# Stick-breaking attention: both heads' logits in one tile of two PSUM banks, weights scaled in halves

## The chip, the core and the metric

The kernel runs on one core of a Trainium2 chip. The metric is the device time of one launch in microseconds. TensorE (PE, with its weight loads as PEld), VectorE (DVE), ScalarE (ACT), GpSimd (POOL) and the DMA-issuing SyncE (SP) run side by side, each through its own queue in order, and wait for each other by semaphores.

## What is computed

A decoder trunk of two layers over 1040 tokens (16 meta tokens and 1024 of the sequence), width 1024, in float32: a Mamba-2 mixer and a gated FFN, then stick-breaking attention and a second gated FFN. The change touches the attention, 16 heads of 64:

```python
kv = _rmsnorm(h, kv_norm) @ w_kv
q = (_rmsnorm(h, sb_norm[j]) @ sb_w_q[j]).reshape(b, L, SB_HEADS, SB_HEAD_DIM)
...
logits = jnp.einsum('bthd,bshd->bhts', q[:, t0:t1], k[:, :t1]).astype(jnp.float32) * scale
visible = s_idx < t_idx
log_keep = jnp.where(visible, jax.nn.log_sigmoid(-logits), 0.0)
later = lax.cumsum(log_keep, axis=3, reverse=True) - log_keep
log_w = jnp.where(visible, jax.nn.log_sigmoid(logits) + later, -jnp.inf)
w = jnp.exp(log_w).astype(v.dtype)
outs.append(jnp.einsum('bhts,bshd->bthd', w, v[:, :t1]))
```

The kernel takes the sums of logarithms as running products: `kp` holds sigmoid(-logit) and is scanned from the right, `bt` holds sigmoid(logit) and is multiplied by the scanned `kp` of its right neighbour.

## The kernel before

Mixer, FFN and output projection are ordered by the framework's scheduler. The attention is written out by hand: on PE, DVE, ACT and POOL its instructions run in program order.

`attention` (L1385) goes through eight **pairs** of heads. A pair has 18 **steps** n = 0 to 17, one for each (i, jj): query block i of 116 tokens against the third jj of the keys (at most 348 columns), jj falling from i//3 to 0. The steps with jj = i//3, on the diagonal, are n = 0, 1, 2, 3, 5, 7, 9, 12 and 15. Steps 0, 3 and 9 have 116 columns, 1, 5 and 12 have 232, all others 344 or 348. In each step:

- `weigh` (L1317) computes the logits: for each of the two heads two matmuls into a PSUM bank of its own, `lg` (L1332; two banks in all). ACT takes from each bank a sigmoid into `kp` (L1335) and one into `bt` (L1336), the first head's two ahead of the second's. On the diagonal POOL masks both (L1341). DVE scans `kp` (L1345) and multiplies `bt` (L1346), head by head. POOL sets one column of each `kp` to 1 (L1329). `kp` has six buffers and `bt` eight, that is three and four steps.
- `half` (L1238) is half a projection: 12 matmuls of the weight tiles `wh`, `wl` against the normed tokens, into `pj` (L155 to L157; two banks, tag `mm`). Steps 0 to 7 project the last third of the pair's own v, q, k, v; steps 8 to 17 the first two thirds of the next pair's k, q, q, k and the first of its v, two steps for each. What reads a finished `pj` comes a step later in program order: for q two copies on ACT (L1279) and two subtractions on DVE (L1283, from `pj`), for k a copy (L1266) and a subtraction (L1267); ahead of these, in the same step, `pj` of k is read by DVE (L1255) and `pj` of v by ACT (L1257).
- A **chore**, where one is due. `load` (L1207) issues the DMA of a weight tile `w32` (128 x 1024) for the next pair at the end of step 4 (k), 7 (q) or 9 (v), and appends two chores, of which each following step runs one. A chore (`some`, L1226) takes half of the tile: four ACT copies with the norm's gain as scale make `wh` (L1233), four DVE operations make `wl` (L1234). Pair 0's own weights go through POOL.
- `flush` (L1398): `turn` (L1350) of the step three back, which transposes the weights `bt` (up to six transposes, L1359, into one of three `sm` banks for each head) and copies them to SBUF on ACT (L1363). When blocks 2b and 2b+1 are complete, `values` (L1365) multiplies with v (`po`, L1374), and ACT copies `po` out (L1381).

The last pair has no next pair to project: from step 8 on its steps hold logits, transposes and values alone, and PE has little to do in them. The eight PSUM banks are: `mm` 2, `lg` 2, `sm` 3, `ex` 1.

Of the kernel before, what the change touches and what calls it, by code (L numbers as in the profile page):

```python
# [68 lines left out]
class Trunk:  # L69
    def __init__(self, ctx, tc, a):  # L70
        self.tc, self.nc, self.a = tc, tc.nc, a
        nc = self.nc
# [4 lines left out]
        self.mp = ctx.enter_context(tc.tile_pool(name="mp", bufs=2, space=bass.MemoryType.PSUM))
        self.sp = ctx.enter_context(tc.tile_pool(name="sp", bufs=SMB, space=bass.MemoryType.PSUM))
        self.dp = ctx.enter_context(tc.tile_pool(name="dp", bufs=1, space=bass.MemoryType.DRAM))
        self.n = 0  # L80
# [14 lines left out]
    def mm(self, s="mm"):  # L95
        return self.mp.tile([P, 512], F32, tag="mm", name=self.nm(s))
# [4 lines left out]
    def lg(self, s="lg"):  # L101
        return self.sp.tile([P, 512], F32, tag="lg", name=self.nm(s), bufs=LGB)
# [1094 lines left out]
    def heads(self, u, p, pool):  # L1197
# [4 lines left out]
        class Pair:  # L1202
# [4 lines left out]
            def load(me, kind):  # L1207
# [18 lines left out]
                def some(k0):  # L1226

                    if k0 == 0:
                        me.w[kind] = [self.wp.tile([P, 1024], F32R, tag=t, name=self.nm(t)) for t in ("wh", "wl")]
                    for k in range(k0, k0 + KD // 2):  # L1230
                        w, wh, wl = (t[:, k * P : k * P + P] for t in (w32, *me.w[kind]))
                        g = self.par(gain, k)
                        nc.scalar.activation(wh, w, AF.Copy, scale=g)  # L1233
                        nc.vector.scalar_tensor_tensor(wl, w, g, wh.bitcast(F32), op0=ALU.mult, op1=ALU.subtract)  # L1234
# [82 lines left out]
    def weigh(self, i, jj, qd, ks, prev, pool):  # L1317
# [6 lines left out]
        out = []  # L1324
        for a in range(2):
            kp = pool.tile([P, TW], F32, tag="kp", name=self.nm("kp"), bufs=6)
            bt = pool.tile([P, TW], F32, tag="bt", name=self.nm("bt"), bufs=8)

            nc.gpsimd.memset(kp[:nt, m : m + 1], 1.0)  # L1329
            ps = self.lg()  # L1330
            for x, part in enumerate(qd[a]):
                nc.tensor.matmul(ps[:nt, :m], part[:, c0 : c0 + nt], ks[a][:, s0 : s0 + m], start=x == 0, stop=x == 1)  # L1332
            out.append((kp, bt, ps))
        for kp, bt, ps in out:
            nc.scalar.activation(kp[:nt, :m], ps[:nt, :m], AF.Sigmoid, scale=self.rt[2][:nt, i : i + 1])  # L1335
            nc.scalar.activation(bt[:nt, :m], ps[:nt, :m], AF.Sigmoid, scale=self.rt[1][:nt, i : i + 1])  # L1336
        for a, (kp, bt, _) in enumerate(out):
            if jj == j:

                for t, fill in ((kp, 1.0), (bt, 0.0)):  # L1340
# [4 lines left out]
            nc.vector.tensor_tensor_scan(rev, rev, self.one[:nt].to_broadcast([nt, m + 1]), init, ALU.mult, ALU.mult)  # L1345
            nc.vector.tensor_tensor(bt[:nt, :m], bt[:nt, :m], kp[:nt, 1 : m + 1], op=ALU.mult)  # L1346
            prev[a] = kp
        return [bt for _, bt, _ in out]
# [185 lines left out]
    def run(self, ctx):  # L1534
        tc = self.tc
        with tc.tile_pool(name="mx", bufs=1) as mx:
            hd, ys, yd = self.mixer(mx)
        self.rp = ctx.enter_context(tc.tile_pool(name="rp", bufs=1))
        with tc.tile_pool(name="ff0", bufs=2) as pool:
            d, *forms = self.out_proj(hd, ys, yd, pool)  # L1540
            g = self.up(0, *forms, pool)
            h1 = self.dp.tile([KD, P, L], F32, tag="h1_d", name="h1_d")

            def to_attention(h, j, u):
                u = self.norm(h, j, u)
                self.spill_tile(h, h1, *TT[j])
                return u

            u = self.down(0, g, d, pool, to_attention)
        with tc.tile_pool(name="att", bufs=2) as pool:  # L1550
# [3 lines left out]
        with tc.tile_pool(name="ff1", bufs=2) as pool:  # L1554
# [65 lines left out]
```

## Time and profile before

| | us |
|---|---|
| median of 3 runs | 2925.82 (2924.74 to 2927.37) |
| the profiled execution | 2925.94 |
| its span, first to last instruction | 2924.2 |
| mixer and first FFN: 0 to 1578 | 1578, PE busy 1534.4, DVE 1109.3, ACT 878.9 |
| attention: 1578 to 2118 | 540, PE busy 517.7, DVE 452.1, ACT 427.5, POOL 129.6 |
| output projection and second FFN: 2118 to the end | 806, PE busy 784.2, DVE 565.6, ACT 392.6 |

Busy times are unions of instructions, and matmuls overlap: two of the same kind start 0.16 us apart and are shown with 0.32 us each. So a stall of PE shows best as a longer distance from one start to the next, or as idle time of PEld, and less as idle time of PE. Timeline rows give start, duration, engine, line, operation and tiles; a number in brackets at the end is the engine's idle time just before, with what ended it.

### The profile page before, as it was taken

What the parts mean: (1) busy time and instruction counts of PE and PEld (TensorE: products, weight loads), DVE (VectorE), ACT (ScalarE), POOL (GpSimd) and SP (SyncE); (2) the same over time, 40 slices, a digit from 0 to 9 for tenths busy, and PEclk for the clock granted to TensorE, in tenths of its full rate; (3) what the DMA queues carried; (4) which work ended last, traced back from release to release, by engine and by line L of the source; (5) the groups of instructions that cost most, each with busy time, mean ns of one, the idle gap of its engine ahead of it and who ended that gap; (6) DMA issues with size and microseconds to landing.
All of it is one profiled execution on the core that took longest, in us unless ns stands there. A gap on an engine that the chain in (4) does not pass through costs nothing.

```text
span 2924.2 us, 57048 instructions
## 1 busy us (share of the span) xinstructions
PE 2836.3 (97%) x21793; PEld 2705.8 (93%) x21793; DVE 2127.0 (73%) x4100; ACT 1699.1 (58%) x3608; POOL 700.9 (24%) x956
## 2 busy tenths in 40 slices
PE   8999999999999999999999999999898999999998
PEld 5999898988998999999998999999797999999888
DVE  5685858776497655558986888888869656557895
ACT  5586667763155555555335888787736555555442
POOL 0000000000005666650002222222200766662000
PEclk9999999999999999999999999999999999999999
DMA  4233333323222222235132222222341222225331
GB/s 166 71 110 93 115 92 106 112 66 135 75 94 66 81 81 78 76 117 198 52 127 72 64 60 64 61 68 54 98 163 48 86 78 80 80 80 188 108 108 59
DMA packets 133570, 272.74 MB, mean 93 GB/s; under 512 B 16400, under 2 KB 68240, under 8 KB 133296
## 3 DMA queue, kind: packets, MB, share of 16 engines
q1 hardware_dynamic: 127984, 258.17, 27.8%
q10 hardware_dynamic: 4048, 6.36, 0.6%
q0 software_dynamic: 1264, 4.57, 0.4%
q8 instruction: 171, 2.80, 0.4%
q14 instruction: 103, 0.84, 0.1%
HBM read 200.93 MB, written 53.21 MB: 87 GB/s over the span
## 4 chain that ended last, share of the span: by engine, by line
PE 65%; DVE 7%; ACT 4%; issue 1%; DMA 1%; ACTq 0%; DVEq 0%; POOL 0%; SPq 0%; POOLq 0%
PE p L155 9%; PE p L157 9%; PE p L156 9%; PE acc L156 8%; PE acc L157 8%; PE acc L155 8%; PE po L1374 2%; PE pj L155 2%; PE pj L157 2%; PE pj L156 2%; PE lg L1332 2%; PE wT L1359 1%; DVE kp L1345 1%; ACT kp L1335 1%; ACT bt L1336 1%
## 5 line engine op out<-in xcount | busy, mean ns | idle before, releaser
L155 PE MATMUL pj<-uh,wh 128*128 128x348 f32 (+2 forms) x1536 | 504.1, 329 | 17.5 <-DVE xbc L278 9.1
L156 PE MATMUL pj<-ul,wh 128*128 128x348 f32 (+2 forms) x1536 | 496.9, 324 | 0.0
L157 PE MATMUL pj<-uh,wl 128*128 128x348 f32 (+2 forms) x1536 | 494.5, 322 | 0.0
L155 PE MATMUL p<-bh,fh 128*128 128x262 f32 (+1 forms) x1408 | 399.1, 284 | 12.3 <-DVE p L969 6.8
L156 PE MATMUL p<-bl,fh 128*128 128x262 f32 (+1 forms) x1408 | 399.5, 284 | 0.9 <-DVE bl L854 0.7
L157 PE MATMUL p<-bh,fl 128*128 128x262 f32 (+1 forms) x1408 | 398.5, 284 | 0.7 <-DVE fl L919 0.7
L155 PEld LDWEIGHTS pj<-uh,wh 128*128 128x128 f32 x1536 | 290.4, 189 | 25.6 <-issue 11.5
L155 PE MATMUL p<-bh,wh 128*128 128x262 f32 (+1 forms) x1056 | 301.0, 285 | 1.9 <-ACT bh L853 1.7
L156 PE MATMUL p<-bl,wh 128*128 128x262 f32 (+1 forms) x1056 | 300.0, 284 | 2.1 <-DVE bl L854 2.1
L157 PE MATMUL p<-bh,wl 128*128 128x262 f32 (+1 forms) x1056 | 299.5, 284 | 0.0
L156 PEld LDWEIGHTS pj<-ul,wh 128*128 128x128 f32 x1536 | 290.9, 189 | 1.0
L157 PEld LDWEIGHTS pj<-uh,wl 128*128 128x128 f32 x1536 | 290.5, 189 | 0.3 <-issue 0.2
L155 PEld LDWEIGHTS p<-bh,fh 128*128 128x128 f32 x1408 | 267.1, 190 | 13.8 <-DVE p L969 7.2
L278 DVE SCALAR_TENSOR_TENSOR c<-p,params,c 128x260 f32<-128x260 f32 (+1 forms) x440 | 208.4, 482 | 92.6 <-ACT c L274 90.8
L156 PEld LDWEIGHTS p<-bl,fh 128*128 128x128 f32 x1408 | 267.2, 190 | 2.5 <-DVE bl L854 2.4
L157 PEld LDWEIGHTS p<-bh,fl 128*128 128x128 f32 x1408 | 266.2, 189 | 1.1 <-DVE fl L919 1.1
L919 POOL TENSOR_TENSOR fl<-x,fh 128x1024 fp32r<-128x1024 f32 x80 | 192.3, 2404 | 246.8 <-ACT fh L918 246.8
L969 DVE TENSOR_TENSOR p<-p,ft 128x262 f32<-128x262 f32 (+1 forms) x176 | 76.4, 436 | 215.6 <-ACT ft L966 123.1
L156 PE MATMUL acc<-gl,wh 128*128 128x260 f32 (+1 forms) x672 | 211.5, 320 | 0.1
L157 PE MATMUL acc<-gh,wl 128*128 128x260 f32 (+1 forms) x672 | 208.8, 320 | 0.0
L155 PE MATMUL acc<-gh,wh 128*128 128x260 f32 (+1 forms) x672 | 204.0, 319 | 0.0
L156 PEld LDWEIGHTS p<-bl,wh 128*128 128x128 f32 x1056 | 200.7, 190 | 3.1 <-DVE bl L854 3.1
(313 smaller groups left out, 7717.3 us busy)
## 6 DMA issues: line engine op xcount, KB each, us to landing
w<-in_w_up SPq DMA_DIRECT2D x88, 512.0 KB
w<-in_w_down SPq DMA_DIRECT2D x44, 512.0 KB
w<-in_w_in SPq DMA_DIRECT2D x40, 512.0 KB
E<-ea_d SPq DMA_DIRECT2D x32, 464.0 KB
D<-acs_d SPq DMA_DIRECT2D x32, 420.5 KB
g<-c SPq DMA_DIRECT2D x88, 130.0 KB
g<-c SPq DMA_DIRECT2D x88, 128.0 KB
b<-g SPq DMA_DIRECT2D x16, 520.0 KB
```

The costliest lines, as they stand in the source:

```text
L155: mm(out, wh, uh, start=first, stop=False, skip_group_check=joins)
L156: mm(out, wh, ul, start=False, stop=False, skip_group_check=joins)
L157: mm(out, wl, uh, start=False, stop=last, skip_group_check=joins)
L278: nc.vector.scalar_tensor_tensor(to, ps[:, o + i : o + i + n], wcol(i), out, op0=ALU.mult, op1=ALU.add)
L919: tt(lo[:, :n], t, hi[:, :n].bitcast(F32), op=ALU.subtract)
L969: add = lambda o, x, y: tt(o[:, :N], x[:, :N], y[:, :N], op=ALU.add)
L1332: nc.tensor.matmul(ps[:nt, :m], part[:, c0 : c0 + nt], ks[a][:, s0 : s0 + m], start=x == 0, stop=x == 1)
L1335: nc.scalar.activation(kp[:nt, :m], ps[:nt, :m], AF.Sigmoid, scale=self.rt[2][:nt, i : i + 1])
L1336: nc.scalar.activation(bt[:nt, :m], ps[:nt, :m], AF.Sigmoid, scale=self.rt[1][:nt, i : i + 1])
L1345: nc.vector.tensor_tensor_scan(rev, rev, self.one[:nt].to_broadcast([nt, m + 1]), init, ALU.mult, ALU.mult)
L1359: nc.tensor.transpose(pt[:ns, x * CB : x * CB + nt], bt[a][:nt, x * CB : x * CB + ns], self.ident[:nt, :nt])
L1374: nc.tensor.matmul(po[64 * a : 64 * a + 64, w], v[: CH[c][1], c, 64 * a : 64 * a + 64], wt[a][: CH[c][1], c, :nt], start=x == 0, stop=x == ...
```

## The change

In the attention `lg` becomes one tile of two banks, `lg2`, with a head in each, and one such tile in place of two banks. One sigmoid for `kp` and one for `bt` now take both heads at once, as do the mask, the column of ones and the product. The two scans stay. `kp` has three double tiles and `bt` four. The chores of pairs 1 to 7 change: the first multiplies the whole weight tile by the gain in place, in two halves on DVE; the second makes `wh` in two ACT copies and `wl` in two DVE subtractions. The load of q moves from step 7 to step 6. In the last pair, from step 9 on, odd steps take a second `lg2` tile, in the two banks that the projections had. To allow this the banks `mm` and `lg` come from pools (`banks`) that are opened for each stage.

```diff
-        self.mp = ctx.enter_context(tc.tile_pool(name="mp", bufs=2, space=bass.MemoryType.PSUM))
...
+    def banks(self):
+        return self.tc.tile_pool(name=self.nm("lp"), bufs=1, space=bass.MemoryType.PSUM)
...
-                def some(k0):
-
-                    if k0 == 0:
-                        me.w[kind] = [self.wp.tile([P, 1024], F32R, tag=t, name=self.nm(t)) for t in ("wh", "wl")]
-                    for k in range(k0, k0 + KD // 2):
-                        w, wh, wl = (t[:, k * P : k * P + P] for t in (w32, *me.w[kind]))
-                        g = self.par(gain, k)
-                        nc.scalar.activation(wh, w, AF.Copy, scale=g)
-                        nc.vector.scalar_tensor_tensor(wl, w, g, wh.bitcast(F32), op0=ALU.mult, op1=ALU.subtract)
-
-                return [lambda: some(0), lambda: some(KD // 2)] if p else [scale, parts]
+                def scale_halves():
+                    for x in range(2):
+                        v = w32[:, D // 2 * x : D // 2 * (x + 1)].rearrange("p (k c) -> p k c", c=P)
+                        g = self.par(gain, KD // 2 * x, KD // 2).unsqueeze(2).to_broadcast([P, KD // 2, P])
+                        nc.vector.tensor_tensor(v, v, g, op=ALU.mult)
+
+                def part_halves():
+                    me.w[kind] = [self.wp.tile([P, 1024], F32R, tag=t, name=self.nm(t)) for t in ("wh", "wl")]
+                    halves = [[t[:, D // 2 * x : D // 2 * (x + 1)] for t in (w32, *me.w[kind])] for x in range(2)]
+                    for w, wh, _ in halves:
+                        nc.scalar.activation(wh, w, AF.Copy)
+                    for w, wh, wl in halves:
+                        nc.vector.tensor_tensor(wl, w, wh.bitcast(F32), op=ALU.subtract)
+
+                return [scale_halves, part_halves] if p else [scale, parts]
...
-        for kp, bt, ps in out:
-            nc.scalar.activation(kp[:nt, :m], ps[:nt, :m], AF.Sigmoid, scale=self.rt[2][:nt, i : i + 1])
-            nc.scalar.activation(bt[:nt, :m], ps[:nt, :m], AF.Sigmoid, scale=self.rt[1][:nt, i : i + 1])
...
+                nc.tensor.matmul(ps[:nt, a, :m], part[:, c0 : c0 + nt], ks[a][:, s0 : s0 + m], start=x == 0, stop=x == 1)
+        for t, r in ((kp, self.rt[2]), (bt, self.rt[1])):
+            nc.scalar.activation(t[:nt, :, :m], ps[:nt, :, :m], AF.Sigmoid, scale=r[:nt, i : i + 1])
...
+        for a in range(2):
+            rev = kp[:nt, a, : m + 1][:, ::-1]
+            init = 1.0 if jj == j else prev[0][:nt, a, 0:1]
             nc.vector.tensor_tensor_scan(rev, rev, self.one[:nt].to_broadcast([nt, m + 1]), init, ALU.mult, ALU.mult)
-            nc.vector.tensor_tensor(bt[:nt, :m], bt[:nt, :m], kp[:nt, 1 : m + 1], op=ALU.mult)
-            prev[a] = kp
-        return [bt for _, bt, _ in out]
+        nc.vector.tensor_tensor(bt[:nt, :, :m], bt[:nt, :, :m], kp[:nt, :, 1 : m + 1], op=ALU.mult)
+        prev[0] = kp
+        return [bt[:, a] for a in range(2)]
...
-        loads = {(-1, 4): "k", (-1, 7): "q", (-1, 9): "v"}
+        loads = {(-1, 4): "k", (-1, 6): "q", (-1, 9): "v"}
...
+        both = lambda p: p.tile([P, 2, 512], F32, tag="lg2", name=self.nm("lg"))
...
+                if p + 1 == PAIRS and n == 9:
+                    mine.close()
+                    more = spare.enter_context(self.banks())
+                ps = both(more if p + 1 == PAIRS and n > 8 and n % 2 else self.lp)
+                bt = self.weigh(i, jj, now[0].qd[i // 3], now[0].ks, prev, pool, ps)
```

What this does to the queues. First DVE, in the third pair, from the first of k's chores in step 5 to the first chore of q; `w` is the weight tile as loaded, `wh` and `wl` its two parts, `klo` the subtraction that follows k's copy. Before:

```order
L1234 SCALAR_TENSOR_TENSOR wl_20095<-w_2760_20038,params,wh_20094 128x128 [waits Activation_49] x3
L1345 SCALAR_TENSOR_TENSOR kp_20126<-kp_20126,kp_20052,one 116x349 [waits Activation_49,Pool_49]
L1346 TENSOR_TENSOR bt_20127<-bt_20127,kp_20126 116x348 [waits DVE_49,PE_49,Activation_49]
L1345 SCALAR_TENSOR_TENSOR kp_20132<-kp_20132,kp_20058,one 116x349 [waits Activation_49,Pool_49]
L1346 TENSOR_TENSOR bt_20133<-bt_20133,kp_20132 116x348 [waits DVE_49,PE_49,Activation_49]
L1267 TENSOR_TENSOR klo_20159<-k_20092,k_18958 128x344 [waits DMAHW2_49,Activation_49]
L1234 SCALAR_TENSOR_TENSOR wl_20095<-w_2760_20038,params,wh_20094 128x128 [waits Activation_49] x4
L1345 SCALAR_TENSOR_TENSOR kp_20181<-kp_20181,one 116x349 [waits Pool_49]
```

After, the same stretch (line numbers are shifted: L1346 is the scan, L1347 the product, L1337 the sigmoids, L1335 the logits):

```order
L1232 TENSOR_TENSOR w_2640_19610<-w_2640_19610,params 128x512 [waits DMAHW1_49]
L1232 TENSOR_TENSOR w_2640_19610<-w_2640_19610,params 128x512
L1346 SCALAR_TENSOR_TENSOR kp_19680<-kp_19680,kp_19625,one 116x349 [waits Activation_49,Pool_49]
L1346 SCALAR_TENSOR_TENSOR kp_19680<-kp_19680,kp_19625,one 116x349
L1347 TENSOR_TENSOR bt_19681<-bt_19681,kp_19680 116x2x348 [waits DVE_49,PE_49,Activation_49]
L1273 TENSOR_TENSOR klo_19705<-k_19653,k_18722 128x344 [waits DMAHW2_49,Activation_49]
L1240 TENSOR_TENSOR wl_19712<-w_2640_19610,wh_19711 128x512 [waits Activation_49] x2
L1346 SCALAR_TENSOR_TENSOR kp_19728<-kp_19728,one 116x349 [waits Pool_49]
```

The two scans now stand next to each other with no wait between them, one product follows, and all of `wl` is made in the second chore, a step later than its first half was.

Then ACT in the same pair, steps 5 and 6; `wt` is the copy of the transposed weights, `o` that of `po`. Before:

```order
L1336 ACTIVATE bt_20059<-lg_20061,rt_17598 116x232
L1233 ACTIVATE wh_20094<-w_2760_20038,params 128x128 [waits DMAHW1_49]
L1233 ACTIVATE wh_20094<-w_2760_20038,params 128x128 x3
L1381 ACTIVATE o_20111<-po_20104 128x116 [waits DMAHW6_49,DMAHW5_49,PE_49]
...
L1335 ACTIVATE kp_20126<-lg_20129,rt_17599 116x348 [waits DVE_49,PE_49]
L1336 ACTIVATE bt_20127<-lg_20129,rt_17598 116x348
L1335 ACTIVATE kp_20132<-lg_20135,rt_17599 116x348 [waits DVE_49,PE_49,Pool_49]
L1336 ACTIVATE bt_20133<-lg_20135,rt_17598 116x348
L1266 ACTIVATE k_18958<-k_20092 128x344 [waits DVE_49]
L1233 ACTIVATE wh_20094<-w_2760_20038,params 128x128 x4
```

After:

```order
L1337 ACTIVATE bt_19626<-lg_19624,rt_17605 116x2x232
L1382 ACTIVATE o_19664<-po_19657 128x116 [waits DMAHW6_49,DMAHW5_49,PE_49]
...
L1337 ACTIVATE kp_19680<-lg_19679,rt_17606 116x2x348 [waits DVE_49,PE_49,Pool_49]
L1337 ACTIVATE bt_19681<-lg_19679,rt_17605 116x2x348
L1272 ACTIVATE k_18722<-k_19653 128x344 [waits DVE_49]
L1238 ACTIVATE wh_19711<-w_2640_19610 128x512 [waits DMAHW1_49,DVE_49]
L1238 ACTIVATE wh_19711<-w_2640_19610 128x512 [waits DVE_49]
```

The first chore has left ACT; the second now waits for DVE's scaling, half by half.

Last PE in a step of the last pair that has no projection, logits, transposes and logits. Before:

```order
L1332 MATMUL lg_25871<-k_24368,qs_25440 116x348 [waits Activation_49]
L1332 MATMUL lg_25871<-k_24368,qs_25440 116x348
L1332 MATMUL lg_25877<-k_24369,qs_25442 116x348 [waits Activation_49]
L1332 MATMUL lg_25877<-k_24369,qs_25442 116x348
L1359 MATMUL wT_25888<-ident,bt_25747 116x116 [waits DVE_49,PE_49]
L1359 MATMUL wT_25888<-ident,bt_25747 116x116 x2
```

After:

```order
L1335 MATMUL lg_24405<-k_23172,qs_24052 116x348 x2
L1335 MATMUL lg_24405<-k_23173,qs_24054 116x348 x2
L1360 MATMUL wT_24418<-ident,bt_24310 116x116 [waits DVE_49,Activation_49]
L1360 MATMUL wT_24418<-ident,bt_24310 116x116 x2
L1360 MATMUL wT_24423<-ident,bt_24310 116x116 [waits Activation_49]
L1360 MATMUL wT_24423<-ident,bt_24310 116x116 x2
```

With the second tile the logits of these steps carry no wait of their own; the transposes wait for the product of both heads. In the pairs before, the first of a step's four logit matmuls waits for ACT's last sigmoid of the step before, and the others for nothing. The order of PE's work in the attention and of all DMAs on SP is otherwise what it was; a few matmuls of the second FFN change places.

More of the change, by code (lines that the diff above doesn't have):

```diff
@@ L95, in mm @@
     def mm(self, s="mm"):
-        return self.mp.tile([P, 512], F32, tag="mm", name=self.nm(s))
+        return self.lp.tile([P, 512], F32, tag="mm", name=self.nm(s), bufs=2)
     def sm(self, s="sm"):
@@ L101, in lg @@
     def lg(self, s="lg"):
-        return self.sp.tile([P, 512], F32, tag="lg", name=self.nm(s), bufs=LGB)
+        return self.lp.tile([P, 512], F32, tag="lg", name=self.nm(s), bufs=LGB)
+    def banks(self):
+        return self.tc.tile_pool(name=self.nm("lp"), bufs=1, space=bass.MemoryType.PSUM)
     def ex(self, s="ex"):
@@ L1241, in half @@
                 if h == 0:
-                    me.ps[kind, j] = self.mm("pj")
+                    me.ps[kind, j] = self.pj.tile([P, 512], F32, tag="mm", name=self.nm("pj"), bufs=2)
                 ps = me.ps[kind, j]
@@ L1323, in weigh @@
         m = min(TT[jj][1], t0 + nt - s0)
-        out = []
+        kp = pool.tile([P, 2, TW], F32, tag="kp", name=self.nm("kp"), bufs=3)
+        bt = pool.tile([P, 2, TW], F32, tag="bt", name=self.nm("bt"), bufs=4)
+        nc.gpsimd.memset(kp[:nt, :, m : m + 1], 1.0)
         for a in range(2):
[L1326 to L1330, printed above, removed]
@@ new lines, in weigh @@
+        for t, r in ((kp, self.rt[2]), (bt, self.rt[1])):
+            nc.scalar.activation(t[:nt, :, :m], ps[:nt, :, :m], AF.Sigmoid, scale=r[:nt, i : i + 1])
+        if jj == j:
+            for t, fill in ((kp, 1.0), (bt, 0.0)):
+                own = t[:nt, :, c0 : c0 + nt]
+                nc.gpsimd.affine_select(out=own, in_=own, compare_op=ALU.is_gt, fill=fill, base=0, pattern=[[0, 2], [-1, nt]], channel_multiplier=1)
+        for a in range(2):
+            rev = kp[:nt, a, : m + 1][:, ::-1]
+            init = 1.0 if jj == j else prev[0][:nt, a, 0:1]
@@ L1443, in attention @@
             flush(0)
+        spare.close()
         return od
@@ L1535, in run, with to_attention @@
         tc = self.tc
[L1536 to L1550, printed above, removed]
+        with self.banks() as self.lp:
+            with tc.tile_pool(name="mx", bufs=1) as mx:
+                hd, ys, yd = self.mixer(mx)
+            self.rp = ctx.enter_context(tc.tile_pool(name="rp", bufs=1))
+            with tc.tile_pool(name="ff0", bufs=2) as pool:
+                d, *forms = self.out_proj(hd, ys, yd, pool)
+                g = self.up(0, *forms, pool)
+                h1 = self.dp.tile([KD, P, L], F32, tag="h1_d", name="h1_d")
+                def to_attention(h, j, u):
+                    u = self.norm(h, j, u)
+                    self.spill_tile(h, h1, *TT[j])
+                    return u
+                u = self.down(0, g, d, pool, to_attention)
+        with tc.tile_pool(name="att", bufs=2) as pool, self.banks() as self.lp:
             E = mybir.EngineType
@@ L1553, in run @@
                 od = self.attention(u, pool)
-        with tc.tile_pool(name="ff1", bufs=2) as pool:
+        with tc.tile_pool(name="ff1", bufs=2) as pool, self.banks() as self.lp:
             d, *forms = self.o_proj(h1, od, pool)
```

16 lines of the change are left out of this document (4 added, 12 removed).

## The prediction

> **What bounds the kernel now.** I read the page's engine row first, then the windows of three stretches of the attention, then the waits of one pair.
>
> ```profile
> PE 2836.3 (97%) x21793; PEld 2705.8 (93%) x21793; DVE 2127.0 (73%) x4100; ACT 1699.1 (58%) x3608; POOL 700.9 (24%) x956
> ...
> 1780.80:1848.20 67.40, 65.52 (x570) 62.40 (x568) 56.97 (x113) 53.77 (x156) 16.00 (x72) 1.00 0.22 60
> 2050.70:2118.00 67.30, 58.70 (x566) 51.73 (x564) 54.51 (x93) 52.36 (x146) 17.85 (x71) 0.97 0.32 102
> ```
>
> The columns of the two windows are length, then busy time of PE, PEld, DVE, ACT, POOL, then PE's clock. The first is a middle pair: PE binds, DVE follows at 85%. The second is the last pair: PEld is busy ten microseconds less and the stretch is no shorter, so something else binds there. Whatever takes work from ACT and DVE is worth, in a middle pair, only the stalls that PE has there. They are these, from PEld's waits (total, times, longest), first for that middle pair, then for the whole attention, then for the last pair:
>
> ```profile
> PEld lg L1332 <- ACT bt L1336: 1.5, 3, 0.6
> PEld pj L155 <- DVE qs L1283: 1.3, 1, 1.3
> PEld po L1374 <- issue: 1.1, 5, 0.2
> ...
> PEld lg L1332 <- ACT bt L1336: 16.8, 32, 0.8
> PEld pj L155 <- DVE qs L1283: 9.3, 7, 1.3
> ...
> PEld lg L1332 <- ACT bt L1336: 7.2, 12, 0.8
> ```
>
> So before the last pair's stretch the logits waited 16.8 - 7.2 = 9.6 us for ACT, and seven projections waited 9.3 us for DVE. Some of this is ordinary turnaround between groups (the `po` row has 0.2 each where PE waits for nothing); I count 9.6 + 9.3 = 18.9 as 17 us of real delay. That is all that the first seven pairs can give.
>
> **ACT.** Rows of ACT in step 6 of the middle pair (start, duration), and of a 116-column step:
>
> ```profile
> 1806.36 0.62 ACT L1335 ACTIVATE kp<-lg,rt 116x348 f32<-116x348 f32 x1
> ...
> 1808.09 0.59 ACT L1266 ACTIVATE k<-k 128x344 fp32r<-128x344 f32 x1
> 1808.47 1.37 ACT L1233 ACTIVATE wh<-w,params 128x128 fp32r<-128x128 f32 x4
> 1809.64 0.51 ACT L1363 ACTIVATE wt<-wT 116x116 f32<-116x116 f32 x2
> 1809.93 0.66 ACT L1335 ACTIVATE kp<-lg,rt 116x348 f32<-116x348 f32 x1
> ...
> 1811.23 0.69 ACT L1336 ACTIVATE bt<-lg,rt 116x348 f32<-116x348 f32 x1
> 1811.66 0.60 ACT L1257 ACTIVATE v<-pj 128x344 f32<-128x344 f32 x1
> ...
> 1817.36 0.37 ACT L1335 ACTIVATE kp<-lg,rt 116x116 f32<-116x116 f32 x1
> 1817.60 0.38 ACT L1336 ACTIVATE bt<-lg,rt 116x116 f32<-116x116 f32 x1
> ```
>
> Four sigmoids of 348 columns take 1808.09 - 1806.36 = 1.73 us, 0.43 each from start to start; one of 116 takes 0.24. That is 0.00083 us a column and 0.14 fixed. A merged one of 696 columns is not in the trace: between 0.72 (one fixed part) and 0.87 (nothing saved). I take 0.72, since the rows fall on a line; the two then take 1.45 for 1.73. A chore of four copies takes 1809.64 - 1808.47 = 1.17; the new pair of 512-column copies, at most the same by the column rate and a fixed part (0.57 each), 1.14, once for each weight instead of twice.
>
> **When the single tile comes free.** The logits of the next step wait until both merged sigmoids end. In PE's rows, with one of PEld at the end:
>
> ```profile
> 1805.44 0.89 PE L1332 MATMUL lg<-k,qs 128*116 128x348 f32 x4
> 1808.16 0.88 PE L1332 MATMUL lg<-k,qs 128*116 128x348 f32 x4
> 1811.29 1.26 PE L1332 MATMUL lg<-k,qs 128*116 128x348 f32 x4
> 1814.38 1.61 PE L1374 MATMUL po<-wt,v 116*64 116x116 f32 x28
> ...
> 1819.53 0.87 PE L1332 MATMUL lg<-k,qs 128*116 128x348 f32 x4
> ...
> 1842.53 0.42 PE L155 MATMUL pj<-uh,wh 128*128 128x348 f32 x1 [1.04 <-DVE qs L1283]
> ...
> 1811.97 0.28 PEld L1332 LDWEIGHTS lg<-k,qs 128*116 128x116 f32 x2 [0.43 <-ACT bt L1336]
> ```
>
> The last logit arrives 0.89 after the group starts, the sigmoids take 1.45, and a sigmoid's result comes up to 0.26 after the next may start (1811.23 + 0.69 = 1811.92 against 1811.66) with 0.05 to the released load at 1811.97: 0.89 + 1.45 + 0.31 = 2.65 us after the group began. The shortest step of a pair with projections is 1808.16 - 1805.44 = 2.72, so a prompt ACT just fits. Where ACT is late: the third group above (1811.29) had to wait 0.38 (1.26 for 0.88). In the changed queue ACT starts at the same 1806.36, does sigmoids 1.45, k 0.38, the chore 1.14, two `wt` 0.29, and sigmoids 1.45 again, released at 1811.38, against 1811.29 wanted: a stall of 0.1 instead of 0.38. The first chore, which stood before 1806.36, is gone from ACT.
>
> **DVE.** Step 6 and the first scan of step 7, the `qs` of step 14, and the pieces that price a 512-column operation:
>
> ```profile
> 1808.28 0.94 DVE L1345 TENSOR_TENSOR_SCAN kp<-kp,kp,one 116x349 f32<-116x349 f32 x1
> 1809.36 0.52 DVE L1346 TENSOR_TENSOR bt<-bt,kp 116x348 f32<-116x348 f32 x1
> 1809.80 0.94 DVE L1345 TENSOR_TENSOR_SCAN kp<-kp,kp,one 116x349 f32<-116x349 f32 x1
> 1810.87 0.52 DVE L1346 TENSOR_TENSOR bt<-bt,kp 116x348 f32<-116x348 f32 x1
> 1811.31 0.59 DVE L1267 TENSOR_TENSOR klo<-k,k 128x344 fp32r<-128x344 f32 x1
> 1811.82 1.17 DVE L1234 SCALAR_TENSOR_TENSOR wl<-w,params,wh 128x128 fp32r<-128x128 f32 x4
> 1812.91 0.87 DVE L1345 TENSOR_TENSOR_SCAN kp<-kp,one 116x349 f32<-116x349 f32 x1
> ...
> 1841.41 1.07 DVE L1283 TENSOR_TENSOR qs<-pj,qs 64x348 fp32r<-64x348 f32 x2
> ...
> 2077.14 0.95 DVE L149 TENSOR_TENSOR wl<-w,wh 128x768 fp32r<-128x768 f32 x1
> 2078.01 0.94 DVE L1345 TENSOR_TENSOR_SCAN kp<-kp,kp,one 116x349 f32<-116x349 f32 x1
> ```
>
> A step is scan to product 1.08, product to scan 0.44, 1.07, 0.44: 3.03 us. A product waits for its scan, but a scan follows the other head's product 0.08 before that has ended (0.52 busy, 0.44 apart). Two scans in a row do not occur in this trace: 0.94 - 0.08 = 0.86 apart if they overlap so, 1.08 if a scan must wait like a product. I take 0.86, as the only neighbours without a wait between them do overlap. The double product saves one fixed part: 768 columns take 0.87, 348 take 0.44, so 0.00102 a column, 0.08 fixed, 0.80 for 696. Sum 0.86 + 1.07 + 0.80 = 2.73, **0.3 less a step** (0.1 without overlap). The fixed parts don't depend on the columns, so I use 0.28 for every step.
>
> The Trainium skill, VectorE: DVE Perf Modes, section "The DRAIN you can't avoid", says that the next operation does not start before the pipe is empty; the two starts above, 0.08 before an end, speak against it here. By it the scans would stand at 0.94 or more and a step would save 0.2.
>
> A weight costs DVE 2 x (1812.91 - 1811.82) = 2.18 now and four operations of 0.61 after: 2.44, 0.26 **more**. POOL could lengthen these; it gets half as many, wider operations, and is not in front of PE anywhere in the waits above.
>
> What is late next on DVE: three things that PE needs.
>
> - `wl` of k, now made entirely in step 6. DVE's first scan of step 4 starts 0.29 later (the merged `kp` takes 0.72, not 0.43), which eats that step's gain; step 5 gains 0.28, the scaling costs 0.13 more than half the old chore, so step 6 starts at about 1808.13, ends at 1810.86, `klo` (0.51) at 1811.37, and the first half of `wl` is there by 1812.1. PE wants it in step 8, after four logits and two matmuls: 1811.38 + 0.72 + 0.32 = 1812.4 (the next matmul starts 0.16 before a group of 0.88 ends; two matmuls 0.16 apart). It fits, by 0.3.
> - `wl` of q: with the load moved a step ahead it is made in step 8. From `klo`'s end at 1811.37: `wl` of k 1.22, two steps of 2.73, the scaling 1.22, half of `wl` with its 0.08 of delay 0.69: 1820.0. PE wants it in step 10, at 1819.53 - 0.3 (the stall gone) + 0.72 + 0.32 = 1820.3. Before that ACT, done with step 8's sigmoids at about 1813.8, waits some 2 us for the scaling's first half (1811.37 + 1.22 + 2.73 + 0.69 = 1816.0); behind the wait stand its two copies, `o`, `wt` and the next, short sigmoids, through by about 1819. PE, with 28 `po` in that step, asks for the tile at 1819.5.
> - `qs` in step 14, for which PE waited. From 1812.91 to 1841.41 lie eight steps (-2.24) and two weights (+0.52), and the start is some 0.3 earlier: it begins at 1839.4 and ends at 1840.5. PE wanted it 1.2 before 1842.53, at 1841.3, and now, with 0.7 of stalls gone before, at 1840.6. The 1.2 us shrink to 0 to 0.1.
>
> So I leave 0.3 us a pair of new or remaining stalls: 17 - 7 x 0.3 = **15 us** from seven pairs. ACT's slack covers its edits (53.77 of 67.40 busy). The DMAs keep their order on SP; q's tile is asked for a step earlier.
>
> **The last pair.** From its step 4 DVE does not rest until the end:
>
> ```profile
> 2070.26 0.95 DVE L1345 TENSOR_TENSOR_SCAN kp<-kp,kp,one 116x349 f32<-116x349 f32 x1 [1.84 <-ACT kp L1335]
> ...
> 2113.07 0.52 DVE L1346 TENSOR_TENSOR bt<-bt,kp 112x348 f32<-112x348 f32 x1
> 2115.12 1.38 DVE L166 TENSOR_TENSOR ol<-o,oh 128x348 fp32r<-128x348 f32 x3 [1.52 <-ACT oh L165]
> ...
> 2113.74 0.47 PE L1359 MATMUL wT<-ident,bt 112*116 112x112 f32 x3 [1.03 <-DVE bt L1346]
> 2114.15 3.61 PE L1374 MATMUL po<-wt,v 116*64 116x112 f32 x36
> ```
>
> PE's last transposes wait for DVE's last product, so the pair ends with DVE: 14 steps x 0.28 = 3.9 sooner, less 0.3 for the later first scan and 0.3 because both heads' transposes now follow the last product: **3.3 us**. PE's and ACT's part (a second tile, 1.45 + 0.7 us of ACT a step) stays below DVE's 2.73. The 36 last `po` take 3.61 where 28 took 1.61 above: the granted clock, 0.97 in the mean of that window, is low here. Whether this falls so again is worth 3.61 - 36/28 x 1.61 = 1.5 to the good; I leave it.
>
> **Sum:** 15 + 3.3 = 18.3 us off the profiled execution's 2925.9 (span 2924.2 and 1.7 around it; the median of the runs is 2925.8, the same): **2907.5 us**.
>
> **Rivals.**
> 1. The single tile keeps PE waiting. If a merged sigmoid saves nothing (0.87), the tile is free 2.94 after the group starts, 0.2 too late in the shortest steps, and ACT is 0.3 later wherever it is late: about 1 us a pair stays. 17 - 7 x 1.2 + 3.3 = 12: 2914. For it: a margin of only 0.07; against it: the ACT rows' straight line. The Trainium skill, Perfetto Trace Analysis, section "Matmuls", says that groups should rotate through banks so that one's evacuation overlaps the next one's matmuls; this change gives that up for seven pairs. By that rule it is this rival; the rows agree only that the margin is thin.
> 2. DVE gains nothing: scans 1.08 apart, 0.07 saved a step, 0.26 lost a weight. Then `qs` is as late as before, `wl` of k and q come 0.3 to 0.4 late, and a pair wins only the logits' 1.3 less 1.0: 7 x 0.3 + 0.3 = 2 us, 2923.
> 3. Slower: the scaling on DVE, in place and with a broadcast operand, costs double (1.2 for 512 columns). Then each `wl` comes at least 1.2 late, k's and q's past PE's margins of 0.3 by 1 to 2 us each, and `qs` 3 us later still: some 5 us of new stalls a pair against the 2.4 gone, 7 x 2.6 - 3 = 15 slower, 2941. It decides from about 0.9 a half. Against it: 768 columns in 0.87.
>
> **Chances.** Forecast 0.70, rival 1 0.12, rival 2 0.13, rival 3 0.05. The forecast's own range is 2902 (all stalls gone, 17 + 3.3, the clock at full for the last `po`) to 2913; with rival 1 the range is 2902 to 2917. 0.2% is 5.9 us, about what a measurement can tell here. Faster by more 0.80 (forecast but for a small rest, and rival 1), within 0.14 (rival 2), slower 0.06.
>
> **What would show it.** Right: the middle pair at about 65.2 us instead of 67.4; no PEld wait on `qs`, logits waiting below 0.4 a pair; merged sigmoids 0.72 apart; scans 0.86 apart. Wrong: a new wait of PE on `wl`, logit waits in most steps, a DVE window as busy as 56.97, the two scans 1.08 apart, POOL in front of DVE, or the last pair ending with ACT.

## The result and the profile after

| | before | after |
|---|---|---|
| median of five runs, us | 2924.74 (2922.09 to 2927.37) | 2909.45 (2908.34 to 2910.47) |
| ratio, with its 95% interval | | 0.9942 (0.9931 to 0.9953) |
| the profiled execution, its span | 2925.94, 2924.2 | 2910.47, 2908.8 |
| one pair (first logits of the second pair to those of the last, by six) | (2050.69 - 1645.61) / 6 = 67.51 | (2038.37 - 1644.49) / 6 = 65.65 |

The change makes the kernel 15.3 us faster; 2907.5 was predicted, and the range of 2902 to 2917 holds the time. The page's engine row of the changed kernel, then a window of one pair's length in the middle and one that begins 6.8 us before the last pair's first logits, in the columns of the prediction's windows:

```profile
PE 2832.3 (97%) x21793; PEld 2703.7 (93%) x21793; DVE 2112.5 (73%) x3872; ACT 1638.0 (56%) x3194; POOL 676.5 (23%) x668
```

```profile
1706.30:1771.90 65.60, 65.45 (x570) 62.44 (x569) 55.41 (x83) 45.91 (x101) 12.95 (x36) 1.00 0.22 62
2031.60:2101.00 69.40, 62.71 (x608) 56.70 (x606) 57.40 (x81) 51.47 (x116) 14.10 (x39) 0.98 0.33 105
```

PE is still what bounds a middle pair, now with hardly a gap. ACT gave up 8 of 54 us, DVE 1.6 of 57. Busy time leaves out the 0.14 us between a scan's end and its product's start, which each step now has once instead of twice, 18 x 0.14 = 2.5 us a pair. With them DVE is 4.1 us shorter, close to the 18 x 0.28 - 3 x 0.26 = 4.3 of the prediction. The waits of the changed kernel over the whole attention (engine, line, what it waited for, total, times, longest):

```profile
ACT wh L1238 <- DVE w L1232: 23.1, 14, 2.5
...
PEld wT L1360 <- DVE v L1304: 5.3, 9, 1.5
...
PEld pj L157 <- DVE qs L1289: 2.0, 7, 0.3
...
PEld lg L1335 <- ACT bt L1337: 1.5, 7, 0.2
...
PEld pj L159 <- DVE wl L1240: 0.4, 1, 0.4
```

The logits' wait for ACT fell from 16.8 to 1.5 us and the wait for `qs` from 9.3 to 2.0. The wait for `v` grew from 2.1 us, once each in the first and the last pair, to 5.3; in the six pairs between it is new, 2.2 us in all. Compared by the start of each step's first logits in the two traces, a middle pair (the fourth) gains 0.63 us at its step 0, 0.37 at step 8, 0.54 at step 12 and 1.00 at step 16. It loses 0.22 in steps 6 and 7, 0.34 in step 10 and 0.21 in step 17, together 1.83 us with the rests. Steps 17 and 0 have to be read together, and so have 7 and 8, 11 and 12: before, it was the second head's logits that waited, inside their step, while with one tile a wait for ACT stands ahead of a step's first logits and is counted in the step before. DVE and ACT in steps 6 to 9 of the third pair of the changed kernel:

```profile
1736.73 1.77 DVE L1346 TENSOR_TENSOR_SCAN kp<-kp,kp,one 116x349 f32<-116x349 f32 x2
1738.64 0.88 DVE L1347 TENSOR_TENSOR bt<-bt,kp 116x696 f32<-116x696 f32 x1
1739.44 0.69 DVE L1273 TENSOR_TENSOR klo<-k,k 128x344 fp32r<-128x344 f32 x1
...
1744.00 1.29 DVE L1232 TENSOR_TENSOR w<-w,params 128x512 f32<-128x512 f32 x2
1745.21 1.78 DVE L1346 TENSOR_TENSOR_SCAN kp<-kp,kp,one 116x349 f32<-116x349 f32 x2
1747.12 0.88 DVE L1347 TENSOR_TENSOR bt<-bt,kp 116x696 f32<-116x696 f32 x1
1747.92 1.66 DVE L1240 TENSOR_TENSOR wl<-w,wh 128x512 fp32r<-128x512 f32 x2
1749.50 0.68 DVE L1346 TENSOR_TENSOR_SCAN kp<-kp,one 116x117 f32<-116x117 f32 x2
1750.29 0.40 DVE L1347 TENSOR_TENSOR bt<-bt,kp 116x232 f32<-116x232 f32 x1
1750.61 0.61 DVE L1304 TENSOR_TENSOR v<-pv,rt 116x256 f32<-116x256 f32 x2
```

```profile
1738.28 0.86 ACT L1337 ACTIVATE kp<-lg,rt 116x696 f32<-116x696 f32 x1
1739.01 0.87 ACT L1337 ACTIVATE bt<-lg,rt 116x696 f32<-116x696 f32 x1
1739.73 0.49 ACT L1263 ACTIVATE v<-pj 128x344 f32<-128x344 f32 x1
...
1744.72 1.24 ACT L1238 ACTIVATE wh<-w 128x512 fp32r<-128x512 f32 x2 [2.19 <-DVE w L1232]
```

Two merged sigmoids are 0.73 and 0.72 apart. A step of DVE takes 1739.44 - 1736.73 = 2.71. But a weight costs it 1745.21 - 1744.00 = 1.21 for the scaling and 1749.50 - 1747.92 = 1.58 for the subtraction: 2.79, where 2.44 was forecast. In step 10 PE's transposes then wait for the bank that `v`'s product still holds; here are the ends of steps 9 and 10:

```profile
1747.41 0.76 PE L1360 MATMUL wT<-ident,bt 116*116 116x116 f32 x6
1748.03 0.90 PE L1335 MATMUL lg<-k,qs 128*116 128x348 f32 x4
...
1750.67 1.12 PE L1360 MATMUL wT<-ident,bt 116*116 116x116 f32 x6
1751.56 0.88 PE L1335 MATMUL lg<-k,qs 128*116 128x348 f32 x4
```

Six transposes take 1.12 for 0.76, and the product ends at 1751.2, behind the second chore of q and the scans of step 9. By the run without masks below the subtraction's higher price is little of what makes it late.

### The profile page after: what moved, and what is told of

Same layout as the page of the kernel before. It is cut to its first block, busy times and chain, and to the rows that moved or that the text cites. A ratio compares the mean times of both kernels' runs of the same rounds, so it can differ in the third digit from the quotient of the medians.

```text
span 2908.8 us, 55758 instructions
## 1 busy us (share of the span) xinstructions
PE 2832.3 (97%) x21793; PEld 2703.7 (93%) x21793; DVE 2112.5 (73%) x3872; ACT 1638.0 (56%) x3194; POOL 676.5 (23%) x668
## 4 chain that ended last, share of the span: by engine, by line
PE 66%; DVE 6%; issue 4%; DMA 1%; ACT 1%; POOL 1%; ACTq 0%; DVEq 0%; SPq 0%; POOLq 0%
PE p L157 10%; PE p L159 10%; PE p L158 10%; PE acc L159 8%; PE acc L158 8%; PE acc L157 8%; PE pj L157 2%; PE pj L159 2%; PE pj L158 2%; PE po L1375 2%; PE lg L1335 2%; PE wT L1360 2%; DVE kp L1346 1%; DVE bl L856 1%; DVE ft L860 1%
```

## Experiments

Time is the median of the runs; the ratio is to the kernel before, run on the same chip (medians 2925.9 to 2926.8 there). A pair's length is taken as in the table above.

| run | us | ratio (95%) | a pair |
|---|---|---|---|
| the change, run again | 2911.39 | 0.9949 (0.9936 to 0.9961) | 65.66 |
| chores and load as before | 2904.14 | 0.9921 (0.9908 to 0.9935) | 64.66 |
| the weights' part alone | 2934.24 | 1.0026 (1.0016 to 1.0037) | 68.70 |
| q's load in step 7 | 2927.41 | 1.0006 (0.9997 to 1.0014) | 68.20 |
| one tile in the last pair | 2913.88 | 0.9955 (0.9942 to 0.9967) | 65.64 |
| DVE head by head | 2926.39 | 0.9999 (0.9990 to 1.0008) | 67.91 |
| a sigmoid for each head | 2912.36 | 0.9952 (0.9939 to 0.9966) | 65.76 |
| `v` first in step 9 | 2911.49 | 0.9948 (0.9935 to 0.9960) | 65.68 |
| no masks (a single run) | 2904.18 | | 64.84 |
| sigmoids merged alone | 2919.11 | 0.9972 (0.9962 to 0.9983) | 66.87 |
| chores as before, POOL helps in the last pair | 2905.71 | 0.9926 (0.9913 to 0.9938) | 64.66 |

**The weights' part undone, and alone.** The changed kernel with the old chores:

```diff
-                return [scale_halves, part_halves] if p else [scale, parts]
+                return [lambda: some(0), lambda: some(KD // 2)] if p else [scale, parts]
...
-        loads = {(-1, 4): "k", (-1, 6): "q", (-1, 9): "v"}
+        loads = {(-1, 4): "k", (-1, 7): "q", (-1, 9): "v"}
```

> The changed kernel with the weights' part undone: chores and q's load as before, double logits tile kept. My theory: the time comes from the merged logits, sigmoids and products; the chores in halves cost DVE 2.6 to 2.8 us a weight in the changed kernel's trace against 2.18 before, so undoing them costs nothing or gains a little: ratio to the kernel before 0.993 to 0.9945, about 2906 to 2910 us, a middle pair 65.2 to 65.6 us, and PE's wait of the transposes on v (0.4 us a pair) gone. Rival: moving the chores' work off ACT was needed too, the logits wait for ACT again in the steps that hold a chore: 0.5 to 1 us more a pair, 2913 to 2917 us.

And the kernel before with the same two places changed the other way:

> The kernel before with the weights' part alone: two banks, four sigmoids and head by head on DVE as before, chores in halves, q's load in step 6. My theory: without the merged operations the dearer chores make DVE later still: wl of q is some 1 us late, qs of q in step 14 another 1 us, against 0.3 of logit waits gained: slower by 5 to 14 us, 2931 to 2940, ratio 1.002 to 1.005. Rival: taking a chore off ACT is what relieves the logits, and this part alone gains: 2918 to 2922 us.

The theory held both times, though the first time fell below its range: 2904.14, 5 to 7 us below the changed kernel. The second, 2934.24, is 8 us above the kernel before. So this half of the change is a loss that the other half covers. With the old chores the fourth pair keeps all four gains (0.65, 0.39, 0.52, 1.28) and loses only 0.07. Of its waits over the attention nothing is left on `qs`, and this on the other two; the two on `v` lie in the first and in the last pair, as before the change:

```profile
PEld wT L1356 <- DVE v L1300: 2.8, 2, 1.5
...
PEld lg L1331 <- ACT bt L1333: 0.2, 1, 0.2
```

**q's load back in step 7**, with the chores in halves:

```diff
-        loads = {(-1, 4): "k", (-1, 6): "q", (-1, 9): "v"}
+        loads = {(-1, 4): "k", (-1, 7): "q", (-1, 9): "v"}
```

> The changed kernel with q's load back in step 7. My theory: the margin of q's wl was only 0.3 us (the half that PE wants at 1814.7 in the fourth pair is ready at 1814.4); a step later it is ready at about 1816.4, so PE waits 1.5 to 2 us a pair in step 10, of which the 0.4 us of waiting for v falls away: 7 x 1.4 = 10 us slower than the changed kernel, 2917 to 2922 us, ratio 0.997 to 0.999, with a row of PE waiting for DVE's wl at 1.5 to 2 us seven times. Rival: the move of the load doesn't matter, 2909 us, ratio 0.994.

The wait came where the theory put it, and it cost 16 to 18 us where 10 were expected. PE in step 10 of the fourth pair, and the windows around it (PE's clock is the third number from the right: 1.00, 0.97, 0.60, 1.00):

```profile
1821.52 0.32 PE L158 MATMUL pj<-ul,wh 128*128 128x348 f32 x1
1823.64 0.55 PE L159 MATMUL pj<-uh,wl 128*128 128x348 f32 x1 [1.81 <-DVE wl L1240]
1823.99 0.49 PE L157 MATMUL pj<-uh,wh 128*128 128x348 f32 x1
1824.28 0.49 PE L158 MATMUL pj<-ul,wh 128*128 128x348 f32 x1
```

```profile
1816.00:1820.00 4.00, 4.00 (x47) 3.85 (x42) 3.87 (x5) 1.73 (x6) 0.98 (x2) 1.00 0.32 123
1820.00:1824.00 4.00, 2.19 (x16) 1.89 (x15) 3.90 (x10) 3.67 (x7) 0.46 (x3) 0.97 0.00 0
1824.00:1828.00 4.00, 4.00 (x20) 3.93 (x20) 3.87 (x7) 0.74 (x3) 0.10 (x1) 0.60 0.48 153
1828.00:1832.00 4.00, 4.00 (x30) 3.98 (x29) 3.06 (x4) 3.81 (x8) 0.00 (x0) 1.00 0.21 49
```

`wl` is 1823.64 - 1821.52 - 0.16 = 1.96 us late; then matmuls stand 0.29 apart instead of 0.16 until the step is over, ten times 0.13 more. The step takes 6.78 us, against 3.48 in the changed kernel. Six of the seven pairs lost 3.4 to 3.8 us there against before, one 2.3. The one pair that lost 2.3 is the sixth, and the only one in which the clock stayed at 1.00 behind the wait. The load one step ahead, whose margin the prediction worked out, is thus worth 16 to 18 us, all of it made necessary by the chores in halves: with the old chores the load stands in step 7 and nothing waits.

**DVE head by head**, all else merged:

```diff
             nc.vector.tensor_tensor_scan(rev, rev, self.one[:nt].to_broadcast([nt, m + 1]), init, ALU.mult, ALU.mult)
-        nc.vector.tensor_tensor(bt[:nt, :, :m], bt[:nt, :, :m], kp[:nt, :, 1 : m + 1], op=ALU.mult)
+            nc.vector.tensor_tensor(bt[:nt, a, :m], bt[:nt, a, :m], kp[:nt, a, 1 : m + 1], op=ALU.mult)
```

> The changed kernel with scan, product, scan, product head by head on DVE, all else merged. My theory: DVE needs 0.28 us more a step; from its idle time in step 4 to q's wl in step 8 that is four to five steps, 1.1 to 1.4 us, against a margin of 0.3: PE waits about 1 us a pair in step 10 for wl, and by the q-at-7 run such a wait also brings a slower clock, up to 1.3 more; the last pair loses its 3.5: 2920 to 2929 us, ratio 0.998 to 1.001. Rival: the earlier release of the logits by ACT carries the gain of the pairs, and only the last pair loses: 2912 to 2914 us.

The time, 2926.39, is as the theory had it, but there is no wait of 1 us for `wl`. There are many short waits instead, here in the attention up to 2090:

```profile
PEld pj L157 <- DVE qs L1289: 11.5, 14, 1.2
...
PEld lg L1335 <- ACT bt L1337: 7.8, 21, 0.4
...
PEld pj L159 <- DVE wl L1240: 3.8, 7, 0.6
```

The same edit on top of the old chores leaves of the change the merged sigmoids, the merged masks and the tiles:

> The run with the old chores (2904 us), and on DVE scan and product head by head as before: of the change only the merged sigmoids, masks and tiles are left. My theory: ACT's part removes the logits' waits in steps 0, 8 and 12, 1.5 us a pair, and DVE's part the wait for qs in step 16, 1.3 us a pair, which comes back here; the last pair is as slow as before: 7 x 1.5 = 10 us faster than before, 2914 to 2918 us, ratio 0.9955 to 0.9975. Rival: with DVE as late as before the transposes and v hold PE up too, and less than half of the 10 us is left: 2920 us or more.

2919.11 lies between the two ranges. 7.5 us are left, and the 15 us down to 2904.14 are DVE's two scans in a row and one product. By its profile 4.0 of the 7.5 lie in the first seven pairs and 3.2 in the last. There the last 36 `po` took 1.95 us instead of 3.61, so half of that 3.2 is the clock.

**A sigmoid for each head** in the double tile:

```diff
         for t, r in ((kp, self.rt[2]), (bt, self.rt[1])):
-            nc.scalar.activation(t[:nt, :, :m], ps[:nt, :, :m], AF.Sigmoid, scale=r[:nt, i : i + 1])
+            for a in range(2):
+                nc.scalar.activation(t[:nt, a, :m], ps[:nt, a, :m], AF.Sigmoid, scale=r[:nt, i : i + 1])
```

> The changed kernel with a sigmoid for each head, 0.43 us apart, in the double tile: both kp sigmoids first, then both bt. My theory: four take 1.73 instead of 1.45 us, so the second bank is free about 0.3 us later and the logits wait again in the short steps, 0.3 to 0.9 us a pair; the last pair is DVE's: 2911 to 2916 us, ratio 0.9947 to 0.9965. Rival 1: each bank is released by its own last sigmoid, so the first head's logits start earlier and nothing is lost: 2909 us. Rival 2: ACT falls behind so that DVE's scans come late too, and most of the gain goes: 2918 us or more.

2912.36: the theory's range, at its lower end, and within the spread of the two sets of runs of the changed kernel (2909.45, 2911.39). A pair is 0.1 us longer. The logits do wait for ACT again, as the theory had it:

```profile
PEld lg L1335 <- ACT bt L1338: 8.3, 30, 0.5
```

But PE then comes later to what it needs of DVE: no wait for `qs` is left, none for `v` in the six middle pairs, and step 10 takes 3.14 us again. So with the chores in halves ACT's saving is worth 1 to 3 us, because by these waits most of what it wins is lost again to DVE. What it is worth with the old chores, where DVE is not late, was not tried.

**`v` first in step 9**:

```diff
+                if n == 9:
+                    now[0].place()
                 bt = self.weigh(i, jj, now[0].qd[i // 3], now[0].ks, prev, pool, ps)
                 todo, late = late, []
-                now[0].place()
+                if n != 9:
+                    now[0].place()
```

> The changed kernel with v's transposes and its product moved ahead of the logits and scans in step 9. My theory: the 0.35 us a pair that step 10 lost against before is PE's wait for the bank that v's product holds, behind DVE's scans; with v first step 10 takes 3.15 us instead of 3.48 in pairs 1 to 7: 7 x 0.35 = 2.4 us faster than the changed kernel, 2907 us, ratio 0.9934. Rival: DVE is late there in any case, and the wait passes to the k or the scans that come 0.5 us later: no gain, 2909 us.

Step 10 did shrink to 3.14 us, and the theory was still wrong: the rival's 2911.49, a pair of 65.68. The wait passed to the next reader of DVE, `qs`, which PE awaited 2.0 us before:

```profile
PEld pj L157 <- DVE qs L1289: 4.3, 7, 0.6
```

So `v` alone is not the cause: DVE is late, and where that shows is a matter of order.

**Why the subtraction takes 0.79 and not 0.61.** In the changed kernel's trace 36 of the 42 subtractions took 0.86 to 0.88 us and had a mask on POOL beside them; the six others took 0.68 and had none (the expectation miscounts by one). The kernel without masks, which leaves out a part of the computation:

```diff
-        if jj == j:
-
-            for t, fill in ((kp, 1.0), (bt, 0.0)):
-                own = t[:nt, :, c0 : c0 + nt]
-                nc.gpsimd.affine_select(out=own, in_=own, compare_op=ALU.is_gt, fill=fill, base=0, pattern=[[0, 2], [-1, nt]], channel_multiplier=1)
```

> The changed kernel without the masks of the diagonal steps (this part of the computation is left out), so that POOL has little to do beside DVE. My theory: in the changed kernel a wl subtraction of 512 columns took 0.87 us whenever a POOL instruction ran beside it (37 of 42) and 0.68 when none did; without the masks it takes 0.68 nearly every time. Rival: its length hangs on something else (what ACT does, where the tiles lie): still 0.87 in most.

DVE's groups in the seven pairs with chores (busy, then mean ns), first of the changed kernel, then without masks:

```profile
L1240 DVE TENSOR_TENSOR wl<-w,wh 128x512 fp32r<-128x512 f32 x42 | 33.7, 841 | 0.0
L1232 DVE TENSOR_TENSOR w<-w,params 128x512 f32<-128x512 f32 x42 | 27.0, 684 | 0.0
```

```profile
L1240 DVE TENSOR_TENSOR wl<-w,wh 128x512 fp32r<-128x512 f32 x42 | 27.0, 684 | 0.0
L1232 DVE TENSOR_TENSOR w<-w,params 128x512 f32<-128x512 f32 x42 | 27.0, 683 | 0.0
```

The theory held: none takes over 0.69, although 14 of them still have POOL's setting of the column of ones beside them. A pair is 0.81 us shorter than in the changed kernel (64.84 for 65.65), most of the 0.99 that the old chores gave; some of it may be DVE's own waits for the masks, which go as well. Most of it is won in steps 16 and 17, 0.5 us a pair. Step 10 still takes 3.33 to 3.53 us, against 3.14 with the old chores. So the masks explain little of the wait for `v`. What is left for it is that the whole of q's weight is now made ahead of `v`'s product, where it was half before, but no run separates this.

**The last pair with one tile**:

```diff
-                ps = both(more if p + 1 == PAIRS and n > 8 and n % 2 else self.lp)
+                ps = both(self.lp)
```

> The changed kernel without the second tile in the last pair. My theory: DVE binds there at 2.7 us a step and one tile comes free 2.65 us after a step's logits, so the last pair loses at most 1 us: 2909 to 2911 us, ratio 0.994 to 0.995. Rival: PE's transposes and values between two steps' logits add to that chain, and the step is set by PE and ACT at 3 us or more: 3 us or more lost, 2912 to 2916 us.

By the times 2.5 to 4.4 us are lost. From step 8 of that pair to its end it is 2.8 against the first profile of the changed kernel, and 3.8 against that of the changed kernel run again, whose last 36 `po` took 1.95 us for 3.04. That is the rival's size, but its mechanism is only half of it. PE near the end, and the windows there:

```profile
2085.08 0.89 PE L1335 MATMUL lg<-k,qs 128*112 128x344 f32 x4 [1.11 <-ACT bt L1337]
...
2087.66 0.89 PE L1335 MATMUL lg<-k,qs 128*112 128x348 f32 x4 [1.30 <-ACT bt L1337]
...
2090.35 1.50 PE L1335 MATMUL lg<-k,qs 128*112 128x348 f32 x4 [1.20 <-ACT bt L1337]
...
2092.94 4.85 PE L1375 MATMUL po<-wt,v 116*64 116x116 f32 x60
```

```profile
2090.00:2094.00 4.00, 3.65 (x22) 3.28 (x24) 3.87 (x6) 3.06 (x7) 0.00 (x0) 0.50 0.38 125
2094.00:2098.00 4.00, 4.00 (x55) 3.85 (x54) 1.61 (x2) 0.35 (x2) 0.00 (x0) 0.70 0.02 8
```

The steps stand 2.58 and 2.69 apart, the 2.65 that the prediction worked out for one tile, and DVE's last scan comes only 0.4 us later than with two. But from the second of three waits of 1.1 to 1.3 us on the clock is 0.50, and 60 `po` take 4.85 us; with two tiles they take 3.20. So at least 1.65 of the 3.8 us is the clock.

**POOL takes the second head's product** in steps 4 to 14 of the last pair, on top of the old chores:

```diff
+        if share:
+            for a, eng in enumerate((nc.vector, nc.gpsimd)):
+                eng.tensor_tensor(bt[:nt, a, :m], bt[:nt, a, :m], kp[:nt, a, 1 : m + 1], op=ALU.mult)
+        else:
+            nc.vector.tensor_tensor(bt[:nt, :, :m], bt[:nt, :, :m], kp[:nt, :, 1 : m + 1], op=ALU.mult)
```

> The run with the old chores, and in steps 4 to 14 of the last pair the second head's product on POOL instead of DVE, to shorten DVE, which sets that pair's end. Theory: DVE saves up to 0.36 us in each of eleven steps, less what POOL's work beside it adds to the scans (0.05 to 0.2 each): 1 to 3 us faster than 2904 us. Rival: a product of 348 columns takes POOL about 1 us (1.3 for 512), and with the masks before it, it comes late for the transposes or lengthens the scans by as much as it saves: no gain, or 1 to 2 us lost.

No gain, as the rival had it. Here too the clock took part: a row and a window of this run, then the row of the run with the old chores alone:

```profile
2086.25 5.29 PE L1375 MATMUL po<-wt,v 116*64 116x116 f32 x60
```

```profile
2086.00:2090.00 4.00, 4.00 (x42) 3.75 (x42) 3.76 (x5) 1.90 (x4) 0.00 (x0) 0.50 0.04 17
```

```profile
2085.57 3.20 PE L1371 MATMUL po<-wt,v 116*64 116x116 f32 x60
```

**The changed kernel once more**, beside the last two:

> The changed kernel itself, to compare it with the old chores on the same chip: 2908 to 2911 us, ratio 0.993 to 0.9955, a middle pair 65.6 us.

2911.39, 0.4 above the expected range, with a pair of 65.66. The version with the old chores is the fastest of all and beats both kernels.

## Why the prediction was right, point by point

- **What could be won.** 17 us in seven pairs were counted. The run with the old chores won 17.54 + 1.20 = 18.7 in its profile from the first logits of the first pair to those of the last. The count was sound, a little low.
- **What would stay.** 0.3 us a pair was left for new waits. Seven pairs gave (2050.69 - 2038.37) - (1581.20 - 1580.86) = 12.0 us instead of 15, so it is (17 - 12.0) / 7 = 0.7 us by the forecast's count and (18.7 - 12.0) / 7 = 1.0 by that of the old chores. The term most at fault is the price of a weight on DVE, 0.61 an operation and 0.26 more a weight. The scaling fits (0.60); the subtraction takes 0.79 beside a mask, so that a weight costs up to 0.6 more. By the run without masks this, with what else the masks do to DVE, is 0.8 us a pair. The prediction did consider that POOL might lengthen these, and set it aside because POOL stood nowhere in front of PE; but a longer DVE operation shows up as a wait for DVE.
- **Three things that PE needs of DVE.** There is a fourth: `v`'s product, which holds a bank of the transposes. The list left it out, though by the run with `v` first listing it would not have changed the sum, since the wait only moves.
- **ACT.** 0.72 between merged sigmoids, 2 us of waiting for the scaling: as forecast (0.73, 2.19). The tile's 2.65 us agreed where it could be seen, in the last pair with one tile. But the larger part of the gain was not ACT's. A sigmoid for each head costs at most 3 us, and the merged sigmoids without DVE's part win 7.5 of the 22 us that they win together with it. In the run with the sigmoids merged alone the logits still waited 6.4 us for ACT in the first seven pairs (9.5 before), and `qs` 8.6: the prediction put the logits' waits down to ACT alone, but most of them went only when DVE was merged too (0.2 us left with the old chores, 1.5 in the changed kernel).
- **DVE.** Scans 0.86 apart, product 0.80, step 2.73: measured 0.83 (the two scans take 1.77, one 0.94), 0.80, 2.71. Rival 2 said that without this gain the time would be 2923; the run with DVE head by head gave 2926. So the price of that gain was about right, and the rival's condition failed.
- **The margin of 0.3 for q's `wl`** was real. In the fourth pair of the changed kernel the first half of `wl` is ready at 1814.4 (1813.52 + 0.87) and PE asks at 1814.7; one step later costs 16 to 18 us. The estimate had no term for the clock behind such a wait.
- **The last pair.** 3.3 forecast; from its first logits to the first matmul of the output projection it takes 2101.03 - 2038.37 = 62.66 us against 2117.68 - 2050.69 = 66.99 before, 4.3 less. Of these 0.6 is its step 0's logits, which waited before and were no part of the 3.3, and 0.6 a better clock for the last 36 `po` (3.04 for 3.61). In the profile of the changed kernel run again the same 36 took 1.95 and the pair 61.59, so the clock alone moves this term by 1.1 us from one execution to the next.
- **Rival 1** fell with 0.73, and with the logits' wait of 1.5 us in all; **rival 3** with 0.60 for the scaling, though a part of its mechanism, longer operations on DVE, is by the run without masks most of what the weights' part lost.
- **Behind the attention** 1.2 us were given back, for which the sum had no term. The framework orders a few matmuls otherwise there, but that is not shown to be the cause: in the run with one tile the order of PE's work behind the attention is that of the kernel before, by names and shapes, and 1.25 us are lost too. The cause stays open.
- **Luck.** Against the forecast's sum the pairs are 3.0 us short and the stretch behind the attention 1.2, while the last pair gives 1.0 too much and the stretch ahead of the attention 0.3. That the errors partly cancel brought the time to 2 us from the forecast.

## What to carry to other kernels

When one engine binds and a second is only just in time for it, an edit is worth what it does to the second engine's latest delivery, and a wait removed in front of one reader passes to the next. So test the halves of a change apart: here merging the heads won 22 us and the weights in halves lost 5 to 7 of them. And price a wait of TensorE above its length, as the clock behind it may be halved for 3.41 us or more.

## What was not expected of the hardware

- **A mask on POOL lengthens some DVE operations beside it.** In the changed kernel the 512-column subtraction took 0.68 or 0.87, nothing between; the 14 scalings that fell beside masks in the run with q's load in step 7 took 0.87 each instead of 0.68. `klo` took 0.70 instead of 0.51 in six of seven pairs, and 0.58 to 0.60 beside the masks of the kernel before, which take one head each; so beside this operation a merged mask is the dearer one. The product of both heads kept its 0.88 to 0.92, `qs`, which reads one operand from PSUM, its 0.50 to 0.52, and setting two columns to 1 on POOL left the subtraction at 0.68 to 0.69. The Trainium skill, SBUF — State Buffer, section "Who interferes with whom", says that a VectorE instruction with two inputs in SBUF contends with a GpSimd instruction that reads SBUF, and not with one that only writes it. The runs agree on the two kinds of POOL work. They show 0.19 us for the subtraction, and none on the product, which has two such inputs as well.
- **The clock after short waits.** After 1.81 us of idle the granted clock was 0.50 for 3.41 us (0.60 in the window of 4 us above), and after the second of three waits of 1.1 to 1.3 it was 0.50 for 6.83; yet in the run with the old chores a wait of 1.84 us before the last transposes was followed by 1.00. The Trainium skill, TensorE: Matmul & The Clock Gate, section "Why this matters for your kernels", asks for no idle gaps over about 3 us; here shorter ones sufficed at times. The traces also show what goes with it. In every trace the clock is either 1.00 or 0.50 and changes only at points a whole number of 3.41 us apart. Of the 1979 such stretches between 1578 and 2105 us, in all thirteen traces, that ran at 1.00, the 13 in which PEld was busy for less than 39% were all followed by 0.50; of the others three were, with 39%, 44% and 45%. In the run with q's load in step 7 the stretch with the fourth pair's wait had PEld busy for 1.32 of its 3.41 us, and 0.50 followed; that with the sixth pair's had 1.50, and 1.00 followed. The 1.84 us of the old chores fell on two stretches, with 1.78 and 2.40. So by these traces the work within a fixed stretch tells what follows, and not the length of one wait; no run varied this alone.
